# Two layers of a hybrid decoder trunk: v, gate and output projections in pairs of column groups, as 2x2 block products with seven multiplications

## The chip, the cores and the metric

The kernel runs on one core of a Trainium2 chip. The metric is the device time of one execution in microseconds. Before the change three runs gave 1668.3, 1667.81 and 1663.36 us. The names of the engines in the profile are PE (TensorE's matmuls), PEld (its weight loads), DVE (VectorE), ACT (ScalarE), POOL (GpSimd) and SP (SyncE, which here only issues DMAs).

## The reference

S = 512 tokens, width 2048, two layers, all float32. Per layer:

```
h   = rms_norm(x, pre_g)
z   = h @ w_in                       # 2048 -> 6656 = 13 groups of 512 columns
rq, rk, rv, rg (768 each), dq, dk, dv, dg (512 each), lx, lg (768 each) = split(z)
A   = retention(rope(rq), rope(rk), rv)    # 6 heads x 128, chunks of 128, then norm
B   = diff_attention(rope(dq), rope(dk), dv)   # 4 heads, causal, then norm
C   = rg_lru(causal_conv4(lx))             # 768 channels
mix = concat(A * silu(rg), B * silu(dg), C * gate(lg))
x   = x + rms_norm(mix @ w_out, post_g)    # 2048 -> 2048 = 4 groups of 512 columns
```

So there are 17 projections of 512 x 2048 by 2048 x 512 per layer, and the mixers between them.

## The kernel before, in words

Each float32 matrix is split into a high part in the float32r format and the rest (`whi`, `wlo` for weights; `hhi`, `hlo` for the normalised input; `mhi`, `mlo` for the mixers' outputs), and a product is three matmuls: high by high, high by low, low by high. K is cut into 16 tiles of 128. A weight chunk holds two of these tiles by 512 columns (a DMA of 512 KB into `raw`); `load_chunk` splits it with one ACT copy (L163) and one DVE subtraction (L164).

A `Pass` is one projection: 8 chunks by 4 PSUM banks, 192 matmuls of 128 x 512 (L208). In form A the weights are stationary and a bank holds 128 columns for all 512 tokens; in form B the activations are stationary and a bank holds 128 tokens by 512 columns. `run_pass` goes chunk by chunk over the banks and finishes the banks one after the other in the last two chunks, so that `evac` of one bank overlaps the next. `ensure` loads chunks ahead, with high priority.

The order of the passes in a layer: dv, dq, dk, three of lx and lg, three of rq and rk, three of rv and rg, dg, then four column groups of the output projection. Layer 1's dv pass begins with two of its four banks (`defer`), and the last column group is done as two halves of two banks each. Work of the mixers is written as generators in the queue `side`; `pump` takes a step of the first of them after every second chunk and bank, `drain` empties the queue ahead of the output projection (`i == 13`). SP issues in program order. For the other engines a list scheduler fixes one order per engine when the kernel is built, and each engine then takes its instructions in that order.

Names that the change touches: `evac_rvg` and `evac_dv` take v and gates from PSUM into tiles that stay in SBUF; `ret_head` is one head of retention, `ret_final` multiplies its output `ro` with the gate `rg` (L713, POOL) and transposes it; `diff_final` does that for differential attention (`dT`, L552); `lru_final` for the recurrence; `evac_y` and `finish` square, scale and add the residual, and transpose blocks of 128 tokens (`hT`) into the next layer's `hhi`, `hlo`; `start_h` and `start_norm` prepare layer 0, with `rstd` on POOL (L317).

Of the kernel before, what the change touches and what calls it, by code (L numbers as in the profile page):

```python
# [23 lines left out]
P = 128  # L24
# [12 lines left out]
NU = 77  # L37
WBUFS = 3
NWARM = 9
NPOOL = 4  # L40
LEAD, SLEAD, RLEAD = 4, 8, 6
DEFER = 3
# [3 lines left out]
C_RQ, C_RV, C_RG, C_DQ, C_DK, C_DV, C_DG, C_LX = 0, 1536, 2304, 3072, 3584, 4096, 4608, 5120  # L46
# [42 lines left out]
class Pass:  # L89
    def __init__(self, form, wsrc, kts, banks, act, evac, defer=False):  # L90
        self.form, self.wsrc, self.kts = form, wsrc, kts
        self.banks, self.act, self.evac, self.defer = banks, act, evac, defer
# [3 lines left out]
def tile_hybrid_trunk(ctx, tc, x, xt, pos, ppar, lamqk, w_in, gw, w_out, postg, cp, cm, out):  # L96
# [31 lines left out]
    xs = dp.tile([S, DM], F32, name="xs")  # L128

# [17 lines left out]
    passes = []  # L147
    chunk_list = []
    chunk_tiles = {}
# [3 lines left out]
    def load_chunk(i):  # L153
        p, c = chunk_list[i]
        raw = wp.tile([P, 2, S], F32, tag="raw", name=nm("raw"))
        hi = wp.tile([P, 2, S], F32R, tag="whi", name=nm("whi"))
        lo = wp.tile([P, 2, S], F32R, tag="wlo", name=nm("wlo"))
        src = p.wsrc[c].rearrange("p (k c) -> p k c", k=2)
        for a, b in (((0, 1), (1, 2)) if i == 0 else ((0, 2),)):
            if i == 0:  # L160
                load_xt(a)
            nc.sync.dma_start(raw[:, a:b, :], src[:, a:b, :])
            last_copy[0] = A.copy(hi[:, a:b, :], raw[:, a:b, :])  # L163
            V.tensor_tensor(lo[:, a:b, :], raw[:, a:b, :], hi[:, a:b, :], op=ALU.subtract)  # L164
        chunk_tiles[i] = (hi, lo)

    def ensure(i):
        while loaded[0] <= min(i, len(chunk_list) - 1):
            with tc.high_priority(HP):
                load_chunk(loaded[0])  # L170
            loaded[0] += 1
# [16 lines left out]
    cbase = [0]  # L188

    def run_pass(p):  # L190
        nb = len(p.banks)
        ps = {b: pb.tile([P, S], F32, tag="big", name=nm("big")) for b in p.banks}
        nch = len(p.kts) // 2
        base = cbase[0]
        cbase[0] += nch
        cnt = {b: 0 for b in p.banks}
        total = len(p.kts) * 3

        def mm(c, b):
            hi, lo = chunk_tiles[base + c]  # L200
            for kk in range(2):
                ah, al = p.act[p.kts[2 * c + kk]]
                for wt, at in ((hi, ah), (hi, al), (lo, ah)):
# [4 lines left out]
                    T.matmul(ps[b], lhsT=lhsT, rhs=rhs, start=(cnt[b] == 0), stop=(cnt[b] == total - 1))  # L208
                    cnt[b] += 1
            if cnt[b] == total:  # L210
                with tc.high_priority(HP):
                    p.evac(b, ps[b])

        order = []
        rest = 0
        if p.defer:
            order += [(c, b) for c in range(DEFER) for b in p.banks[:2]]
            order += [(c, b) for b in p.banks[2:] for c in range(DEFER)]
            rest = DEFER
        tail = nch - (2 if nb == 4 else 3)  # L220
        for c in range(rest, tail):
            order += [(c, b) for b in p.banks]
        for b in p.banks:
            order += [(c, b) for c in range(tail, nch)]
        for n, (c, b) in enumerate(order):
            ensure(base + max(c, n // nb) + 2)
# [3 lines left out]
        for c in range(nch):  # L230
            del chunk_tiles[base + c]
# [294 lines left out]
    def evac_dv(st):  # L526
        def f(tb, ps):
            t = U("dv")
            A.activation(t, ps, AF.Identity, scale=rstd[:, tb:tb + 1])
            st["dv"][tb] = t  # L530
        return f

# [12 lines left out]
    def diff_final(l, st):  # L545
# [3 lines left out]
        for h in range(DIFF_H):  # L549
# [3 lines left out]
            hi, lo = U("mhi", F32R), U("mlo", F32R)  # L553
            A.activation(hi, ps, AF.Identity, scale=subg[:, l:l + 1])
            V.scalar_tensor_tensor(lo, ps, subg[:, l:l + 1], hi, op0=ALU.mult, op1=ALU.subtract)
            st["mix"][6 + h] = (hi, lo)
# [89 lines left out]
    def lru_final(st):  # L646
        for t in range(LRU_T):
            m = st["lh"][t]
            V.tensor_tensor(m, m, st["lg"][t], op=ALU.mult)
            hi, lo = U("mhi", F32R), U("mlo", F32R)  # L650
            A.copy(hi, m)
            V.tensor_tensor(lo, m, hi, op=ALU.subtract)
            st["mix"][10 + t] = (hi, lo)
# [3 lines left out]
    def ret_head(l, st, h):  # L657
        q, k, v = st["rq"][h], st["rk"][h], st["rv"][h]
# [44 lines left out]
        del st["rq"][h], st["rk"][h], st["rv"][h]  # L703
# [6 lines left out]
    def ret_final(st, heads):  # L710
        for h in heads:
            o = st["ro"].pop(h)
            G.tensor_tensor(o, o, st["rg"][h], op=ALU.mult)  # L713
# [3 lines left out]
            hi, lo = U("mhi", F32R), U("mlo", F32R)  # L717
            A.copy(hi, ps)
            V.tensor_tensor(lo, ps, hi, op=ALU.subtract)
            st["mix"][h] = (hi, lo)  # L720
# [3 lines left out]
    def evac_rvg(st, items):  # L724
        def f(tb, ps):
            gl = [j for j, (kind, h) in enumerate(items) if kind == "g"]
            if gl:
# [322 lines left out]
```

## Time and profile before

| | |
|---|---|
| three runs | 1668.3, 1667.81, 1663.36 us (median 1667.81) |
| the profiled execution: its own time, its span | 1666.37 us, 1664.4 us |
| mean granted TensorE clock | 0.993 |
| PE, PEld busy | 1634.2 us (98%), 1349.5 us (81%) |
| DVE, ACT, POOL busy | 928.7 us (56%), 626.0 us (38%), 259.1 us (16%) |
| DMA | 177.50 MB, mean 107 GB/s |

The span is the time from the first to the last instruction. Busy times of PE come from matmuls that overlap in its pipeline, so the distance from start to start in the chain of waits prices a matmul better than the mean duration of its group. In a row of a tile's view three numbers stand for shortest, median and longest duration in ns. In a row of the stretch view each engine's busy us is followed by its number of instructions, then come the granted clock, the share of DMA engines busy and GB/s.

### The profile page before, as it was taken

To read this page: it belongs to the slowest core of one execution; us is meant where nothing else is said; L and a number is where in the kernel's file an instruction comes from. 1 tells how busy PE (TensorE), PEld (TensorE's weight loads), DVE (VectorE), ACT (ScalarE), POOL (GpSimd) and SP (SyncE) were. 2 spreads that over 40 slices of the span, in tenths; PEclk is the share of its full clock that TensorE was granted. 3 is DMA by queue.
4 is the path that set the end of the run, shared out by engine and by line. 5 is a ranking of instruction groups with operands and counts; after the bars stand their busy time and mean duration, and the time that the engine had idled before them with its cause. 6 is when DMAs were issued, how large, how long until landed. Compare 5 with 4: busy or idle time off the path is not lost. (4 is left out here: it accounts for less than half of the span.)

```text
span 1664.4 us, 19440 instructions
## 1 busy us (share of the span) xinstructions
PE 1634.2 (98%) x7541; PEld 1349.5 (81%) x7541; DVE 928.7 (56%) x1474; ACT 626.0 (38%) x966; POOL 259.1 (16%) x216
## 2 busy tenths in 40 slices
PE   9999899999999999999999998999999999999997
PEld 7788788787877888888888887888888888888886
DVE  6767765665674444322772776664677544442336
ACT  6232345457212323222662224346541222332233
POOL 0011400111261110000110131003035301100003
PEclk9999999999999999999999999999999999999999
DMA  7233222232322222344643222222323322223635
GB/s 258 79 92 101 89 64 84 89 96 76 102 76 77 76 89 83 107 146 158 222 159 100 89 89 77 76 84 83 92 86 102 101 73 77 91 96 108 196 124 199
DMA packets 54747, 177.50 MB, mean 107 GB/s; under 512 B 6656, under 2 KB 7680, under 8 KB 54656
## 3 DMA queue, kind: packets, MB, share of 16 engines
q1 hardware_dynamic: 52592, 169.94, 32.2%
q0 software_dynamic: 1920, 6.29, 1.0%
q8 instruction: 59, 0.97, 0.2%
q14 instruction: 32, 0.26, 0.1%
q10 hardware_dynamic: 144, 0.04, 0.0%
HBM read 167.86 MB, written 8.39 MB: 106 GB/s over the span
## 5 line engine op out<-in xcount | busy, mean ns | idle before, releaser
L164 DVE TENSOR_TENSOR wlo<-raw,whi 128x1024 fp32r<-128x1024 f32 (+1 forms) x289 | 370.5, 1286 | 426.7 <-ACT whi L163 412.8
L163 ACT CAST whi<-raw 128x1024 fp32r<-128x1024 f32 (+1 forms) x289 | 302.6, 1049 | 630.2 <-PE big L208 549.1
L208 PE MATMUL big<-hhi,whi 128*128 128x512 f32 x1024 | 402.9, 394 | 1.5 <-DVE lx L635 1.5
L208 PE MATMUL big<-hhi,wlo 128*128 128x512 f32 x1024 | 400.6, 391 | 1.6 <-DVE wlo L164 1.6
L208 PE MATMUL big<-hlo,whi 128*128 128x512 f32 x1024 | 400.0, 391 | 0.0
L208 PE MATMUL big<-whi,hhi 128*128 128x512 f32 x640 | 255.3, 401 | 3.7 <-ACT rv L738 2.6
L208 PE MATMUL big<-wlo,hhi 128*128 128x512 f32 x640 | 252.0, 395 | 2.7 <-DVE wlo L164 2.7
L208 PE MATMUL big<-whi,hlo 128*128 128x512 f32 x640 | 251.6, 393 | 0.0
L208 PEld LDWEIGHTS big<-hhi,wlo 128*128 128x128 f32 x1024 | 192.9, 188 | 42.5 <-DVE wlo L164 2.0
L208 PEld LDWEIGHTS big<-hhi,whi 128*128 128x128 f32 x1024 | 193.0, 188 | 41.7 <-DVE lx L635 2.0
L208 PEld LDWEIGHTS big<-hlo,whi 128*128 128x128 f32 x1024 | 193.0, 189 | 38.8
L208 PE MATMUL big<-wlo,mhi 128*128 128x512 f32 x512 | 199.5, 390 | 0.6 <-DVE wlo L164 0.6
L208 PE MATMUL big<-whi,mlo 128*128 128x512 f32 x512 | 199.8, 390 | 0.0
L208 PE MATMUL big<-whi,mhi 128*128 128x512 f32 x512 | 199.8, 390 | 0.0
L208 PEld LDWEIGHTS big<-wlo,hhi 128*128 128x128 f32 x640 | 121.5, 190 | 29.4 <-DVE wlo L164 3.1
L208 PEld LDWEIGHTS big<-whi,hhi 128*128 128x128 f32 x640 | 121.5, 190 | 28.3 <-ACT rv L738 3.0
L208 PEld LDWEIGHTS big<-whi,hlo 128*128 128x128 f32 x640 | 121.6, 190 | 24.2
L208 PEld LDWEIGHTS big<-wlo,mhi 128*128 128x128 f32 x512 | 96.1, 188 | 21.2 <-DVE wlo L164 1.5
L208 PEld LDWEIGHTS big<-whi,mlo 128*128 128x128 f32 x512 | 96.2, 188 | 19.7
L208 PEld LDWEIGHTS big<-whi,mhi 128*128 128x128 f32 x512 | 96.1, 188 | 19.6
L773 POOL TENSOR_TENSOR ry<-sy,mhalf 128x1 f32<-128x1 f32 x8 | 4.7, 585 | 406.7 <-DVE sy L771 406.7
L471 ACT ACTIVATE pr<-sc,mx 128x128 f32<-128x128 f32 (+3 forms) x64 | 33.3, 525 | 75.7 <-DVE mx L468 75.6
(212 smaller groups left out, 1530.0 us busy)
## 6 DMA issues: line engine op xcount, KB each, us to landing
raw<-in_w_in SPq DMA_DIRECT2D x207, 512.0 KB, 3.6
raw<-in_w_out SPq DMA_DIRECT2D x80, 512.0 KB, 3.5
xT<-in_xt SPq DMA_DIRECT2D x16, 256.0 KB, 6.6
xr<-in_x SPq DMA_DIRECT2D x16, 256.0 KB, 5.5
xs<-y POOLq DMA_DIRECT2D x16, 256.0 KB, 3.5
xr<-xs SPq DMA_DIRECT2D x16, 256.0 KB, 5.5
pg<-in_postg SPq DMA_DIRECT2D x8, 256.0 KB, 3.9
out<-y POOLq DMA_DIRECT2D x8, 256.0 KB, 4.5
```

Of the source, the lines that this page charges most:

```text
L163: last_copy[0] = A.copy(hi[:, a:b, :], raw[:, a:b, :])
L164: V.tensor_tensor(lo[:, a:b, :], raw[:, a:b, :], hi[:, a:b, :], op=ALU.subtract)
L208: T.matmul(ps[b], lhsT=lhsT, rhs=rhs, start=(cnt[b] == 0), stop=(cnt[b] == total - 1))
L471: A.activation(p[:, :n], sc[c][:, :n], AF.Exp, bias=mx[:, c:c + 1], scale=0.125, accum_out=sums[:, h:h + 1])
L773: G.tensor_tensor(st["ry"][tb], ms, mhalf[:, :1], op=ALU.pow)
```

## The change

Two column groups of 512 with the same activations form a `Pair`: (dv, rv heads 0 to 3), (rg heads 0 to 3, rv and rg of heads 4 and 5), and in w_out (0, 1) and (2, 3); two input and two output pairs per layer, eight in all. For a pair the product is seen as 2 x 2 blocks: the activations by halves of tokens (256) and of K (1024), the weights by halves of K and the two column groups. Seven block products are made in place of eight, in the order of `UNITS`: A11 B11, A12 B21, S1 T1, S2 T2 and S4 B22 taken by turns, S3 T3, A22 T4, each in four chunks of two K tiles. A unit is one chunk of one product for two banks of 128 tokens: 12 matmuls. S1 to S4 are sums of activation blocks, T1 to T4 sums of weight blocks.

The weight sums are made on the way in (`load_pair_unit`): the first K tile of a chunk is added on POOL (L220), the second on DVE, and then split in halves of 128 x 512. The activation sums are made by `Sums.make`: per sum and chunk two additions of 128 x 256 (four where a block is there only as high and low part) and the low part's subtraction on POOL (L364 to L367, L382), the high part on ACT (L381), and both go to DRAM (from ACT's and POOL's DMA queues, L384) and are read back by SP ahead of each unit that needs them, once in each of the two pairs that share them. For layer 1's input the first of the four sums per chunk is made on DVE. The products are combined from PSUM on DVE, with copies c1 and c5 on ACT.

Around it: all passes of the mixers are reordered (layer 0: dq, the two input pairs, dk, three of lx and lg, three of rq and rk by pairs of heads, dg, the two output pairs; layer 1 begins with the two input pairs), v and gates of the pairs go through DRAM (`vg`) and are read back per head, the next layer's input is transposed by halves of tokens (`turn`), NU falls from 77 to 75 tiles, and raw weights get 4 buffers in place of 3. `defer` and the halved last column group are gone.

The diff, cut to its core:

```diff
+A11_B11, A12_B21, S1_T1, S2_T2, S4_B22, S3_T3, A22_T4 = range(7)
+UNITS = ([(A11_B11, c) for c in range(4)] + [(A12_B21, c) for c in range(4)] + [(S1_T1, c) for c in range(4)]
+         + [(s, c) for c in range(4) for s in (S2_T2, S4_B22)]
+         + [(S3_T3, c) for c in range(4)] + [(A22_T4, c) for c in range(4)])
...
+    def load_pair_unit(p, s, c):
...
+            sums = U("sh", F32R), U("sl", F32R)
...
+                nc.sync.dma_start(sums[part].bitcast(F32), p.sums.dram[SUM_OF[s], c, part])
...
+                raw = load_raw(w2[c] if s == S1_T1 else w2[c + 4] if s == S2_T2 else w1[c + 4])
...
+                for kk in range(2):
+                    (G, V)[kk].tensor_tensor(p.x[c][kk], p.x[c][kk], raw[:, kk, :], op=ALU.add)
+            for kk in range(2):
+                split(hi[:, kk, :], lo[:, kk, :], p.x[c][kk])
...
+            raw, more = load_raw(w2[c]), load_raw(w2[c + 4])
+            for kk in range(2):
+                (G, V)[kk].tensor_tensor(raw[:, kk, :], raw[:, kk, :], more[:, kk, :], op=ALU.add)
+                split(hi[:, kk, :], lo[:, kk, :], raw[:, kk, :])
...
+    def run_pair(p, begin=()):
...
+            if s == A11_B11:
+                c1[t] = U("c1")
+                A.copy(c1[t], x)
+            elif s == A12_B21:
+                e = U("e")
+                V.tensor_tensor(e, x, c1[t], op=ALU.add)
+                o1(t, e)
...
+            elif s == S2_T2:
+                V.tensor_tensor(c1[t], x, c1[t], op=ALU.subtract)
+                V.tensor_tensor(c5[t], c5[t], c1[t], op=ALU.add)
...
+        for n, (s, c) in enumerate(UNITS):
...
+            ensure(base + n + 3)
...
+            pump(2)
...
+        def make(self, c, n, eng):
...
+            hi, lo = U("sfh", F32R), U("sfl", F32R)
+            A.copy(hi, t)
+            eng.tensor_tensor(lo, t, hi, op=ALU.subtract)
+            for part, (q, x) in enumerate(((nc.scalar, hi), (nc.gpsimd, lo))):
+                q.dma_start(self.dram[n, c, part], x.bitcast(F32))
...
+    def mixed(l, st, k, m):
...
+        if all(n in st["mf"] for n in (2 * c, 2 * c + 1, 2 * c + 8, 2 * c + 9)):
+            side.appendleft(st["sums_out"].chunk(c, G))
...
+    def start_sums():
+        for c in range(4):
...
+            st["sums_in"].make(c, 0, G)
+            yield
+        yield from st["sums_in"].rest(G)
...
-            side.append(chain(start_norm(), lead(LEAD), tables(), layer_params(0), layer_params(1), ready()))
+            side.append(chain(start_norm(), start_sums(), tables(), layer_params(0), layer_params(1), ready()))
...
-            if i == 13:
+            if i >= 11:
                 drain()
```

How this moves instructions, at three places. First POOL's order early in layer 0. Before, `rstd` is followed by small powers of the parameters (L334, L346) and the first rotary product of dq:

```order
L317 TENSOR_TENSOR rstd<-ms_429,mhalf 128x4
L334 TENSOR_TENSOR e_868<-two_865,dots_846 128x2
L346 TENSOR_TENSOR u_899<-two_865,na_895 128x6
L334 TENSOR_TENSOR e_982<-two_979,dots_962 128x2
L405 TENSOR_TENSOR qk_806<-qk_806,cos_d 128x512
```

After, behind `rstd` (row 13) come 64 rows of the 16 activation sums; here are the last five of them and the first two weight additions of the first pair (`sf` is a sum, `sfl` its low part, `wx` a weight tile, `raw` the other chunk):

```order
L367 TENSOR_TENSOR sf_834<-xT_179 128x256
L384 DMA sums_in_81<-sfl_829 128x512
L367 TENSOR_TENSOR sf_834<-xT_185 128x256
L382 TENSOR_TENSOR sfl_838<-sf_834,sfh_837 128x512
L384 DMA sums_in_81<-sfl_838 128x512
L220 TENSOR_TENSOR wx_523<-wx_523,raw_849 128x512
L220 TENSOR_TENSOR wx_539<-wx_539,raw_887 128x512
```

The first weight addition of the first pair moved behind all 16 sums of the layer's input.

Second, TensorE at the start of the output projection of layer 0. Before, the last transposes of differential attention (`dT`) stand next to the first matmuls of the first column group, and nothing of retention is left:

```order
L552 MATMUL dT_5090<-cmt,dod_1822 128x128
L552 MATMUL dT_5090<-cmt,dod_2020 128x128
L552 MATMUL dT_5090<-cmt,dod_2286 128x128
L208 MATMUL big_5110<-whi_4997,mhi_3433 128x512
L208 MATMUL big_5110<-whi_4997,mlo_3434 128x512
L208 MATMUL big_5110<-wlo_4998,mhi_3433 128x512
L208 MATMUL big_5110<-whi_4997,mhi_3456 128x512
L208 MATMUL big_5110<-whi_4997,mlo_3457 128x512
L208 MATMUL big_5110<-wlo_4998,mhi_3456 128x512
```

After, in the first output pair, between the last matmuls of its second unit, stand retention of heads 2 to 5 and the transposes `rT` of the heads before (`kv`, `ro`, `rs`, `rk` are retention's products):

```order
L345 MATMUL big_5865<-whi_5336,mlo_4863 128x512
L876 MATMUL kv_5466<-rvg_5451,kn_5464 128x128 x3
L887 MATMUL ro_5474<-rvg_5451,sT_5462 128x128 x2
L345 MATMUL big_5865<-wlo_5337,mhi_4862 128x512
L890 MATMUL ro_5474<-rst_5470,qk_4705 128x128
L887 MATMUL ro_5474<-rvg_5451,sT_5462 128x128
L890 MATMUL ro_5474<-rst_5470,qk_4705 128x128
L887 MATMUL ro_5474<-rvg_5451,sT_5462 128x128
L890 MATMUL ro_5474<-rst_5470,qk_4705 128x128
L919 MATMUL rT_5495<-cmt,ro_5135 128x128 x4
L919 MATMUL rT_5509<-cmt,ro_5236 128x128 x4
L862 MATMUL rs_5578<-qk_4995,qk_5009 128x128 x4
```

The mixers' last work moved from earlier passes into the first units of the output pair.

Third, POOL ahead of the output projection of layer 0. Before, the gate products (L713) are followed by the first power of the output norm:

```order
L713 TENSOR_TENSOR ro_4261<-ro_4261,rg_4690 128x512
L713 TENSOR_TENSOR ro_4364<-ro_4364,rg_4692 128x512
L713 TENSOR_TENSOR ro_4491<-ro_4491,rg_4694 128x512
L713 TENSOR_TENSOR ro_4572<-ro_4572,rg_4696 128x512
L773 TENSOR_TENSOR ry_6060<-sy_6058,mhalf 128x1
L800 DMA xs<-y_5318 128x512
```

After, the sums of the last chunk of mixer outputs (`mf`) and then the first weight addition of the output pair, with 66 rows from the gate powers of heads 2 and 3 (row 206) up to it:

```order
L382 TENSOR_TENSOR sfl_5820<-sf_5816,sfh_5819 128x512
L367 TENSOR_TENSOR sf_5825<-mf_5759 128x256
L384 DMA sums_out_83<-sfl_5820 128x512
L367 TENSOR_TENSOR sf_5825<-mf_5770 128x256
L382 TENSOR_TENSOR sfl_5829<-sf_5825,sfh_5828 128x512
L384 DMA sums_out_83<-sfl_5829 128x512
L220 TENSOR_TENSOR wx_5322<-wx_5322,raw_5956 128x512
L220 TENSOR_TENSOR wx_5338<-wx_5338,raw_5982 128x512
```

The weight addition moved behind the last activation sum of the operand.

More of the change, by code (lines that the diff above doesn't have):

```diff
@@ L36 @@
 EPS = 1e-6
-NU = 77
+NU = 75
 WBUFS = 3
+RBUFS = 4
 NWARM = 9
@@ L144, in tile_hybrid_trunk, with load_raw @@
     A.activation(ones, ones, AF.Identity)
-    passes = []
-    chunk_list = []
-    chunk_tiles = {}
+    units = []
+    unit_tiles = {}
     loaded = [0]
     last_copy = [None]
[L153 to L165, printed above, removed]
+    def load_raw(src):
+        raw = wp.tile([P, 2, S], F32, tag="raw", name=nm("raw"), bufs=RBUFS)
+        nc.sync.dma_start(raw, src.rearrange("p (k c) -> p k c", k=2))
+        return raw
@@ new lines, in split_tiles, with split, load_first @@
+    def split_tiles():
+        return (wp.tile([P, 2, S], F32R, tag="whi", name=nm("whi")),
+                wp.tile([P, 2, S], F32R, tag="wlo", name=nm("wlo")))
+    def split(hi, lo, raw):
+        last_copy[0] = A.copy(hi, raw)
+        V.tensor_tensor(lo, raw, hi, op=ALU.subtract)
+    def load_first(p):
+        src = p.wsrc[0].rearrange("p (k c) -> p k c", k=2)
+        raw = wp.tile([P, 2, S], F32, tag="raw", name=nm("raw"), bufs=RBUFS)
+        hi, lo = split_tiles()
+        for a in range(2):
+            load_xt(a)
+            nc.sync.dma_start(raw[:, a:a + 1, :], src[:, a:a + 1, :])
+            split(hi[:, a:a + 1, :], lo[:, a:a + 1, :], raw[:, a:a + 1, :])
+        return hi, lo
@@ L207, in mm @@
                         lhsT, rhs = at[:, b * P:(b + 1) * P], wt[:, kk, :]
-                    T.matmul(ps[b], lhsT=lhsT, rhs=rhs, start=(cnt[b] == 0), stop=(cnt[b] == total - 1))
-                    cnt[b] += 1
-            if cnt[b] == total:
+                    T.matmul(ps[b], lhsT=lhsT, rhs=rhs, start=(c == kk == n == 0), stop=(c == 7 and kk == 1 and n == 2))
+            if c == 7:
                 with tc.high_priority(HP):
                     p.evac(b, ps[b])
[L214 to L224, printed above, removed]
+        order = [(c, b) for c in range(6) for b in range(4)]
+        order += [(c, b) for b in range(4) for c in (6, 7)]
         for n, (c, b) in enumerate(order):
-            ensure(base + max(c, n // nb) + 2)
+            ensure(base + max(c, n // 4) + 2)
             mm(c, b)
@@ L234, in tile_hybrid_trunk, with halves @@
+    def halves(x):
+        return x[:, :256], x[:, 256:]
     cos_r = const.tile([P, S], F32, name="cos_r")
@@ L864, in tile_hybrid_trunk @@
[L864 to L871 removed]
+            (A_(G_LX, ev_l(st, 0)), [lambda st=st, l=l: lru_half(l, st, 0)]),
@@ L877, in tile_hybrid_trunk @@
         layer_passes.append(seq)
         for p, _ in seq:
-            passes.append(p)
-            for c in range(len(p.kts) // 2):
-                chunk_list.append((p, c))
+            for u in (UNITS if isinstance(p, Pair) else range(8)):
+                units.append((p, u))
     st = states[0]
```

403 lines of the change are left out of this document (273 added, 130 removed).

## The prediction

> **What bounds the kernel now.** I read the busy table first, then the chain of waits, then the stretch views and the groups of the engines that the change loads.
>
> ```profile
> span 1664.4 us, 19440 instructions
> PE 1634.2 (98%) x7541; PEld 1349.5 (81%) x7541; DVE 928.7 (56%) x1474; ACT 626.0 (38%) x966; POOL 259.1 (16%) x216
> 1203.45 122.41 PE big L208 x540
> 1325.85 0.89 PE rs L661 x8
> 0.00:1664.40 1664.40, 1529.79 (x6528) 0.99 0.33 107
> PE big L208 <- DVE wlo L164: 4.9, 4, 2.7
> ```
>
> The reader sees an engine that hardly waits. The second line is the whole span; the third is a piece of the chain of waits in which 540 projection matmuls follow each other, 122.41/540 = 0.2267 us from start to start (their own durations overlap, so the mean of a group is no price). The fourth prices the small 128x128 matmuls: 0.89/8 = 0.11. The fifth is the projection matmuls alone, 6528 of them: 6528 x 0.2267 = 1480 of the 1664 us. The longest kind of wait for a split weight costs 4.9 us in all. So TensorE is the bound, and a matmul taken away is worth 0.2267 us, as long as the engines that feed it stay ahead. DVE has 44% free, POOL 84%.
>
> **Removed: matmuls.** A pair of column groups took 2 x 192 matmuls and now takes 28 units of 12, that is 336. Eight pairs: 8 x 48 = 384 fewer; the order of the instructions shows 6144 instead of 6528, and all other TensorE rows as before. Gain: 384 x 0.2267 = 87.1 us. A unit is 12 x 0.2267 = 2.72, a pair 76.2. Weight loads stay under the matmuls as now.
>
> **Added: what feeds them.** The prices:
>
> ```profile
>   L164 DVE TENSOR_TENSOR wlo<-raw,whi x289: 684/1225/2321, 6.5 to 1648.9; 128x1024 fp32r<-128x1024 f32 x144, 128x512 fp32r<-128x512 f32 x1
> L439 DVE TENSOR_TENSOR qk<-big,rsb x40: 677/691/692, 92.9 to 1280.3; 128x512 f32<-128x512 f32 x40
> L400 DVE TENSOR_TENSOR rt<-qk,sin_r x24: 686/1666/1692, 424.7 to 1297.2; 64x512 f32<-64x512 f32 x24
> L401 POOL TENSOR_TENSOR qk<-qk,cos_r x24: 1288/1746/2342, 425.5 to 1300.0; 128x512 f32<-128x512 f32 x24
> L404 DVE TENSOR_TENSOR rt<-qk,sin_d x64: 678/682/690, 107.3 to 996.3; 32x512 f32<-32x512 f32 x64
> L258 DVE SCALAR_TENSOR_TENSOR ang<-turn,ang 128x512 f32<-128x512 f32 x18 | 12.4, 691 | 0.5
> L316 DVE TENSOR_SCALAR ms<-dss 128x4 f32<-128x4 f32 x8 | 1.4, 169 | 0.3
> L713 POOL TENSOR_TENSOR ro<-ro,rg x12: 1282/1291/1306, 564.7 to 1438.1; 128x512 f32<-128x512 f32 x12
> L697 POOL TENSOR_TENSOR rf<-rss,mhalf x12: 1007/1008/1019, 522.1 to 1406.3; 128x4 f32<-128x4 f32 x12
> L800 POOL DMA_DIRECT2D xs<-y x16 | 9.0, 561 | 16.9 <-DVE hlo L813 11.5 <-DVE y L797 5.4
> L584 ACT CAST xh<-xc 128x512 fp32r<-128x512 f32 x12 | 7.4, 620 | 18.9 <-DVE xc L582 18.9
> 52.46 1.03 POOL L317 TENSOR_TENSOR rstd<-ms,mhalf 128x4 f32<-128x4 f32 x1 [6.67 <-DVE ms L316]
> ```
>
> In rows with three numbers these are shortest, median and longest in ns. A 128x512 operation of DVE is 0.69, of POOL 1.29, a POOL DMA issue 0.56, an ACT copy 0.62. A 128x256 POOL addition is in no row: half of 1.29 is 0.65, the smallest POOL tensor operation that works on 4 columns is 1.01; I take 0.70, since it is nearer to half of the row of its own kind, and keep 0.65 and 1.01 as ends.
>
> One activation sum (`make`) is then two additions of 0.70, a wait for ACT's copy (0.62 and a hand-over, 0.8 together), a subtraction of 1.29, and a DMA issue of 0.56: 4.05 us on POOL; with the copy hidden behind the neighbouring sum's additions 3.25. There are 16 per operand and four operands. POOL also adds half of each weight sum, and POOL takes its instructions in the order shown: **the first weight addition of a pair stands behind all activation sums that precede it.** The splits of that unit on ACT and DVE, and so TensorE's S1 matmul, wait for it; behind SP's reads of the sums stand the weight loads of the later units. This is what decides, place by place.
>
> *(1) Layer 0, first pair.* The 16 sums can start when the pow of the last row above ends, 53.5 us. 16 x 4.05 = 65, so 118; addition, copy and subtraction (1.29 + 0.62 + 0.69) give S1 at 121.
>
> ```profile
> L208 PE MATMUL big<-hhi,wlo x1024: 387/389/628, 57.8 to 1279.2; 128*128 128x512 f32 x171
> 40.00:90.00 50.00, 48.56 (x211) 40.03 (x210) 35.88 (x55) 14.63 (x22) 4.04 (x3) 0.93 0.28 88
> 740.00:790.00 50.00, 50.00 (x222) 41.44 (x221) 15.27 (x21) 13.11 (x21) 0.00 (x0) 1.00 0.49 162
> ```
>
> The first pass ends where the second begins, at 57.8, and the eight units before S1 last 21.8: TensorE could take S1 at 79. It waits 42 (29 with 3.25 per sum: 53.5 + 52 + 2.6 = 108). From S1 on DVE has, by the order, 16 weight additions (11), 36 half splits of 0.684 (25), 14 evacuations of 0.69 (10), the angle tables (18 x 0.691, and 10 others, 20 in all), 69 small ones of 0.17 to 0.2 (13) and the rotary rows of four heads (16 x 0.682 and more, 19): 98, 102 with hand-overs, against 20 units of 2.72 = 54: 47 more. Together 89; the low end is 56 (29, and 27 if the tables move into the stall). The second row shows that this stretch had DVE at 35.88 of 50 us before; there is little cover.
>
> The L400 row gives the upper end. Alone that operation takes 686 ns, but its median is 1666, with POOL's L401 beside it (which itself goes from 1288 to 1746), while the operation fed from PSUM (L439) has 677, 691 and 692. So each meeting may cost DVE 1.666 - 0.686 = 0.98, and the order puts about 20 POOL operations into this stretch: 20 more, 109. I take none of it, since the splits' median (1225 for two halves of 684) shows no such cost, and keep 20 for the range. The Trainium skill, "SBUF — State Buffer", section "Who interferes with whom", calls it an exclusive lock: DVE's second port is POOL's only one, and one of the two holds it for a whole instruction. The L400 row agrees with that. By that rule the term would be 20 x 1.29 = 26 higher and the sum 1912.
>
> *(2) The first output pair, in both layers.* Before, the last heads' work lay between the projection matmuls of 13 earlier passes and was hidden. Now retention of heads 2 to 5, their products with the gate and the transposes of the differential heads stand in TensorE's order between the first 24 big matmuls, and POOL must do, ahead of the first weight addition: 8 rotary products and sums and 6 gate products and 12 split halves (26 x 1.29 = 33.5), 24 half-width additions (16.8), 4 pow (4.0), 12 DMA issues (6.7): 61. With the hand-overs to TensorE, ACT and DVE of twelve sums and of four heads that follow one another (12 x 0.8 and four heads' matmul, ACT, DVE, pow rounds of 5 to 6 us) S1 starts 94 after the pair does; TensorE has 21.8 of units and about 100 small matmuls x 0.11 = 11, so 33. It waits 61, of which I take 55, for what POOL can start during the pass before; ends 40 (no hand-overs) and 63. Two layers: 110 (80 to 126).
>
> *(3) Second output pair, layer 0.* In S3 and A22 DVE has 25.4 and 12.4 (evacuations, y, transposed blocks of the next layer) against 14.5 and 10.9 of TensorE: 12 (5 to 20).
>
> *(4) Layer 1's first pair.* It has no pass ahead of it any more. Its activation sums need the last token's rows; four are made on DVE, the other 12 on POOL with four half additions each: 48 x 0.70 + 12 x 1.29 + 12 x 0.56 = 56, hand-overs 10, begun 25 after the last output matmul (DVE has y and the low parts of the last two blocks of tokens first), and 2.6: S1 at 93, where TensorE, whose first 8 units need only the first half of the tokens, could take it at 26 (21.8 and the transposes). 67, of which I take 60, since the first of the twelve needs only the first of DVE's four (45 to 75). Before, the first pass of the layer begins with two banks (`defer`), and TensorE had work there in 9.65 of 10 us:
>
> ```profile
> 815.00:825.00 10.00, 9.65 (x49) 7.67 (x48) 9.13 (x18) 8.55 (x23) 2.77 (x5) 1.00 0.91 327
> ```
>
> *(5) Within the eight pairs.* S3 loads two chunks and a sum per unit, 1.57 MB in 2.72 us, 578 GB/s.
>
> ```profile
> 15.00:20.00 5.00, 5.00 (x24) 4.14 (x23) 4.73 (x7) 4.11 (x7) 0.00 (x0) 1.00 1.04 398
> ```
>
> The busiest stretch moved 398 GB/s. Four such units need 15.8 instead of 10.9 us; the lead of two to three units covers about half: 3 per pair, 24 (0 if the lead covers all, 56 if the splits too run late).
>
> *(6) The ends.* The last two blocks of tokens come only 6 matmuls apart, so DVE's and SP's rows after the last matmul grow by 4 (0 to 6). After each long wait TensorE's clock falls: the second window row above has 0.93 granted after a short idle at 49 to 54 us, 0.07 x 50 = 3.5 us; with four long waits up to 14; I take 8, since part of a slow stretch falls on matmuls that wait anyway (0 to 20).
>
> At nothing: ACT's 858 to 1225 instructions (626 to about 815 us of a longer span; the cover is its idle half); the v and gate rows through DRAM (read one head ahead); the transposes by halves of tokens, same count.
>
> Sum, against the profiled execution's own time 1666.4 (its span and 2.0; 1.4 below the median of the runs): 1666.4 - 87.1 + 89 + 110 + 12 + 60 + 24 + 4 + 8 = **1886**. Low ends: 1666.4 - 87.1 + 56 + 80 + 5 + 45 = 1765. High ends: 1666.4 - 87.1 + 109 + 126 + 20 + 75 + 56 + 6 + 20 = 1991.
>
> **Rivals.** *Throttled throughout:* DVE and POOL exclude each other in all pairs. By the order, the two have 108 us of instructions in layer 1's second output pair against 76 of TensorE, 102 against 80 in layer 0's, 82 and 79 against 76 in the second input pairs, and 20 more in (1): 32 + 22 + 6 + 3 + 20, less the 12 already counted = 71, so 1957. For it: L400's median; the page just named would make it the rule. Against it: TensorE's waits of (1) to (4) leave DVE time to catch up.
> *The waits are small:* POOL's sums fit beside the units before S1, with hand-overs hidden and half additions at 0.65. Then the low ends hold: about 1765.
> *Faster:* the sums are done in time at all four starts, since POOL would begin them as soon as their tiles are there, in the passes before; then only (5) and (6) stand: 1666.4 - 87.1 + 36 = 1615. For it: POOL is 84% idle. Against it: the order, in which the sums stand last ahead of the weight additions, and in (1) the tile that starts them ends at 53.5. It decides where the four starts cost less than 51 together.
> That matmuls are not removed is excluded by the order's count.
>
> **How the numbers follow.** Sum as worked out 0.70; throttled 0.14; small waits 0.10; faster 0.05; a balance near nothing 0.01. The range reaches from the low ends, 1765, to the throttled case and a little over, 1975; the likeliest case alone spans about 1820 to 1945. What can be told from no change is 0.3%, 5 us. Slower 0.94, same 0.01, faster 0.05.
>
> **What would show it.** 6144 big matmuls at 0.227 outside the waits; TensorE waits of 40 us and more at the first S1 of the first input pair, twice at the first output pair and once at layer 1's start, released by a split that in turn waited for POOL; POOL busy without a gap ahead of each; activation sums of about 4 us each; DVE at 90% and over in the first pair's last 20 units. Wrong I would be if TensorE reaches S1 in step with POOL, if a 128x256 POOL addition took well under 0.65, or if the weight waits sit evenly in all units.

## The result, and the profile after

The changed kernel takes 2003.61 us (median of 4 runs, 2002.0 to 2006.66) against 1665.59 us for the kernel before on the same chip: ratio 1.2032, 95% interval 1.2001 to 1.2064. Slower, as forecast, but 118 us more than the 1886 that was forecast and 29 above the range's end. (Some later comparisons have another median for the kernel before, 1663 to 1666.) The page of the changed kernel, its span, busy times and the granted clock:

```profile
span 2000.4 us, 21327 instructions
PE 1633.0 (82%) x7157; PEld 1312.9 (66%) x7157; DVE 1291.3 (65%) x1902; ACT 795.7 (40%) x1297; POOL 681.5 (34%) x636
PE   9636798999999973599752889999999999438894
PEclk9768799999999996699876899999999999768997
```

TensorE is busy 82% of a longer span, and the last two rows (busy tenths and granted clock in 40 slices of 50 us) show where it is not: slices 2 to 5, 15 to 17, 20 to 23, 35 to 36 and the last. These are layer 0's first input pair, its first output pair, the change of layers with layer 1's first input pair, layer 1's first output pair, and the end.

The place is found by TensorE's matmul starts. The time from a stage's first projection matmul to the next stage's first, less 0.2267 for each big and 0.112 for each small matmul in it, is what TensorE stopped or ran slow there (to within some 1 us):

| us lost | before | changed | forecast |
|---|---|---|---|
| layer 0, first input pair (P1) | | 103 | 92 |
| second input pairs, both | | 22 | 6 |
| first output pairs, both (O1) | | 175 | 116 |
| second output pairs, both (O2) | | 39 | 18 |
| layer 1, first input pair | | 89 | 63 |
| whole kernel, without the tail | 55 | 470 | |

(The forecast's 3 us per pair for loads is counted in each row.) Of the 415 us lost more, 384 x 0.2267 = 87 come back by the matmuls saved, and the tail after the last matmul grew by 9: 337, where the spans differ by 2000.4 - 1664.4 = 336.

The three kinds of stop are seen in the waits. TensorE in the first output pair of layer 0 (us in total, times, longest; from 724 to 834), and in layer 1's first pair (1007 to 1122):

```profile
PE rs L862 <- POOL qk L583: 23.1, 1, 23.1
PE big L345 <- ACT whi L188: 16.8, 1, 16.8
PE dT L755 <- ACT mf L757: 13.6, 1, 13.6
...
PE big L345 <- ACT whi L188: 49.6, 2, 42.6
PE rsb L552 <- DVE rb L551: 13.3, 2, 9.4
```

In layer 0's first pair POOL's order does what was forecast. From the timeline of POOL in layer 0 (start, duration, instruction, idle time before): the first and the last sums of the layer's input, and the first weight addition.

```profile
47.87 1.03 POOL L494 TENSOR_TENSOR rstd<-ms,mhalf 128x4 f32<-128x4 f32 x1 [7.94 <-DVE ms L493]
48.87 1.40 POOL L367 TENSOR_TENSOR sf<-xT,xT 128x256 f32<-128x256 f32 x2
51.00 1.28 POOL L382 TENSOR_TENSOR sfl<-sf,sfh 128x512 fp32r<-128x512 f32 x1 [0.73 <-ACT sfh L381]
...
115.55 1.26 POOL L382 TENSOR_TENSOR sfl<-sf,sfh 128x512 fp32r<-128x512 f32 x1 [0.73 <-ACT sfh L381]
117.10 0.56 POOL L384 DMA_DIRECT2D sums_in<-sfl  x1 [0.30 <-POOL sfl L382]
117.68 1.27 POOL L220 TENSOR_TENSOR wx<-wx,raw 128x512 f32<-128x512 f32 x1
```

16 sums from 48.87 to 117.66 are 4.30 each (forecast 4.05). But ACT's order holds too, which was not forecast. ACT in the first output pair, at its last sums: each cast `sfh` waits 3.31 us for POOL's additions, and the weight casts `whi`, whose data was there, follow only behind the last of them (of their four tiles two had landed by 812.8, the others by 818.1 and 822.6).

```profile
816.34 0.62 ACT L381 CAST sfh<-sf 128x512 fp32r<-128x512 f32 x1 [3.31 <-POOL sf L367]
816.99 0.33 ACTq L384 DMA_DIRECT2D sums_out<-sfh  x1
820.26 0.62 ACT L381 CAST sfh<-sf 128x512 fp32r<-128x512 f32 x1 [3.31 <-POOL sf L367]
820.91 0.33 ACTq L384 DMA_DIRECT2D sums_out<-sfh  x1
824.19 0.62 ACT L381 CAST sfh<-sf 128x512 fp32r<-128x512 f32 x1 [3.31 <-POOL sf L367]
824.84 0.33 ACTq L384 DMA_DIRECT2D sums_out<-sfh  x1
825.20 2.18 ACT L188 CAST whi<-wx 128x512 fp32r<-128x512 f32 x4 [0.40 <-ACT sfh L381]
```

SP is a third queue of this kind already here: it could load those tiles only from 806.4 to 819.6, since it waited for tiles that were still being written to DRAM as sums (first row; 755 to 825). And in this pair POOL's order is not what holds the first weight addition: POOL was done at 827 and then idle for 10.43 us, until the weights came (second row).

```profile
SPq L214 <- DMA sums_out<-sfh: 16.2, 4, 4.5
837.43 1.28 POOL L220 TENSOR_TENSOR wx<-wx,raw 128x512 f32<-128x512 f32 x1 [10.43 <-DMA raw<-in_w_out]
```

### The profile page after: what moved, and what is told of

Same layout as the page of the kernel before. It is cut to its first block, busy times and chain, and to the rows that moved or that the text cites. A ratio compares the mean times of both kernels' runs of the same rounds, so it can differ in the third digit from the quotient of the medians.

```text
span 2000.4 us, 21327 instructions
## 1 busy us (share of the span) xinstructions
PE 1633.0 (82%) x7157; PEld 1312.9 (66%) x7157; DVE 1291.3 (65%) x1902; ACT 795.7 (40%) x1297; POOL 681.5 (34%) x636
## 5 line engine op out<-in xcount | busy, mean ns | idle before, releaser
L345 PE MATMUL big<-whi,sh 128*128 128x512 f32 x512 | 212.6, 415 | 116.7 <-ACT whi L188 113.3
L189 DVE TENSOR_TENSOR wlo<-wx,whi 128x512 fp32r<-128x512 f32 x256 | 217.2, 877 | 108.8 <-ACT whi L188 105.6
L188 ACT CAST whi<-wx 128x512 fp32r<-128x512 f32 x256 | 150.1, 618 | 204.1 <-DVE wx L220 120.9
L345 PE MATMUL big<-wlo,sh 128*128 128x512 f32 x512 | 208.0, 417 | 26.7 <-DVE wlo L189 26.4
L220 POOL TENSOR_TENSOR wx<-wx,raw 128x512 f32<-128x512 f32 x96 | 144.4, 1510 | 215.6 <-DMA raw<-in_w_out 118.7
L345 PE MATMUL big<-whi,sl 128*128 128x512 f32 x512 | 208.8, 408 | 0.0
L345 PEld LDWEIGHTS big<-whi,sh 128*128 128x128 f32 x512 | 101.8, 199 | 146.2 <-ACT whi L188 123.1
L345 PEld LDWEIGHTS big<-whi,sl 128*128 128x128 f32 x512 | 102.0, 199 | 21.3
L381 ACT CAST sfh<-sf 128x512 fp32r<-128x512 f32 x64 | 39.6, 619 | 186.2 <-POOL sf L367 127.1
L345 PE MATMUL big<-whi,mhi 128*128 128x512 f32 x192 | 77.3, 403 | 33.7 <-ACT whi L188 33.7
L382 POOL TENSOR_TENSOR sfl<-sf,sfh 128x512 fp32r<-128x512 f32 x60 | 79.9, 1331 | 69.8 <-ACT sfh L381 69.7
L345 PE MATMUL big<-whi,hhi 128*128 128x512 f32 x192 | 80.6, 420 | 23.7 <-ACT whi L188 23.6
L220 DVE TENSOR_TENSOR wx<-wx,raw 128x512 f32<-128x512 f32 x96 | 84.3, 878 | 23.5 <-DMA raw<-in_w_in 23.5
```

The costliest lines, as they stand in the source:

```text
L188: last_copy[0] = A.copy(hi, raw)
L189: V.tensor_tensor(lo, raw, hi, op=ALU.subtract)
L220: (G, V)[kk].tensor_tensor(p.x[c][kk], p.x[c][kk], raw[:, kk, :], op=ALU.add)
L345: T.matmul(ps[s, t], lhsT=at, rhs=wt[:, kk, :], start=(c == kk == m == 0), stop=(c == 3 and kk == 1 and m == 2))
L381: A.copy(hi, t)
L382: eng.tensor_tensor(lo, t, hi, op=ALU.subtract)
```

## The experiments

Theory A: the activation sums, slow and serial on POOL, hold the weights through queues that take their instructions in order. Rivals: DVE and POOL lock each other and that alone makes the waits; the sums' way through DRAM or the DMA rate; the reordering of the mixers. Times of the experiments are medians of 2 runs (the last: 4), beside the kernel before on the same chip.

**Weight sums on DVE.**

```diff
-                    (G, V)[kk].tensor_tensor(p.x[c][kk], p.x[c][kk], raw[:, kk, :], op=ALU.add)
+                    (V, V)[kk].tensor_tensor(p.x[c][kk], p.x[c][kk], raw[:, kk, :], op=ALU.add)
```

> The changed kernel with all weight sums on DVE, none on POOL. Theory (the activation sums in POOL's queue hold the weight sums behind them, and ACT's copies of those sums hold the weight casts): the single waits of 23 us (layer 0) and 43 us (layer 1) at the first S1 shrink to under 10 and 25, since the additions no longer stand behind the 16 sums; the first output pairs keep their 87 us each, because there TensorE stops before S1; DVE gets 128 more operations of 0.68 = 87 us and is late more often inside the pairs. Sum 1950 to 1990. Rival (POOL and DVE lock each other, and that is what makes all waits): DVE's durations fall to their undisturbed values and the waits inside all pairs shrink, under 1930. Rival (the sums' way through DRAM is late, not the additions): the first S1 waits stay at 23 and 43, 2000 to 2060.

1966.03, in the expected range, but not in the expected way: the first S1 still waited 20.7 and 40.8 us, and the weight casts stood on ACT behind `sfh`, though their additions were done. In layer 0 (DVE's two additions, ACT's last sum, the two casts of these weights):

```profile
103.94 2.36 DVE L220 TENSOR_TENSOR wx<-wx,raw 128x512 f32<-128x512 f32 x2 [9.53 <-DMA raw<-in_w_in]
116.03 0.62 ACT L381 CAST sfh<-sf 128x512 fp32r<-128x512 f32 x1 [3.31 <-POOL sf L367]
117.10 1.14 ACT L188 CAST whi<-wx 128x512 fp32r<-128x512 f32 x2 [0.45 <-ACT sfh L381]
```

So POOL's order alone is not the holder. Nor is it the exclusion of DVE and POOL alone (that rival had under 1930). The gain of 38 is spread over all eight pairs. DVE's splits of weight sums in the changed kernel (behind the bar: busy us and mean ns):

```profile
L189 DVE TENSOR_TENSOR wlo<-wx,whi 128x512 fp32r<-128x512 f32 x256 | 217.2, 877 | 108.8 <-ACT whi L188 105.6
```

and in this run:

```profile
L189 DVE TENSOR_TENSOR wlo<-wx,whi 128x512 fp32r<-128x512 f32 x256 | 177.6, 723 | 108.4 <-ACT whi L188 105.1
```

256 x (877 - 723) = 39 us of DVE went with POOL's weight additions. The Trainium skill, "SBUF — State Buffer", section "Who interferes with whom", has a DVE instruction with two SBUF inputs and a POOL instruction that reads SBUF exclude each other. The means agree with that, though the median split of the changed kernel is 683 ns: only some operations meet. That 39 is near the gain of 38 is no proof: the additions themselves also became shorter (means of 1510 ns on POOL, 706 on DVE in this run), and the two were not separated.

**No activation sums; then no sums at all.** The arithmetic of the sums is left out, the copies, writes, reads and loads stay. The lines show the core of the edit to the activation sums:

```diff
-                    minus(t[:, cols], a21, a22)
...
-            A.copy(hi, t)
-            eng.tensor_tensor(lo, t, hi, op=ALU.subtract)
+            for kk in range(2):
+                a = f[2 * c + kk][n % 2]
+                A.copy(hi[:, kk * 256:(kk + 1) * 256], a[0] if isinstance(a, tuple) else a)
```

> Leaves out the arithmetic of the activation sums: high and low part are both a plain ACT copy of one activation block; the writes to DRAM, the reads and the weight sums stay. Theory: the waits at the start of the four pairs shrink to what DVE and the mixers' own chain need: first input pair 98 to 50, first output pairs 87 to 25 each, layer 1's first pair 89 to 35, in all 2004 - 48 - 124 - 54 = 1778 (1730 to 1840). Rival (the way through DRAM and the DMA traffic): above 1950. Rival (port lock in all pairs): the inner waits (S3, A22) shrink as well, the starts stay.

> As the one before, and the weight sums are left out too (their chunks are still loaded): seven products on unsummed blocks. Theory: what is left is 6144 matmuls, the splits, the combinations and the reordered mixers: another 50 to 70 us less, 1690 to 1730, of which 1580 would be the span without any wait that the kernel before does not have. If under 1640, the sums are all there is to pay; if it stays above 1750, the reordering of the mixers and the combinations cost by themselves.

1876.71 and 1779.80. Both above what was expected. Without activation sums P1 loses 73 and O1 123 in all; without any sums P1 50, O1 105, layer 1's first pair 31, the second input pairs 2 in all, none of it in S3. In the first of these runs S1 is held for only 8.5 and 9.6 us in the first input pairs though the way through DRAM is still there, so that way is not the holder. The sums' arithmetic costs 2003.6 - 1779.8 = 224, with all that it made wait, and about 200 remain above 1580. The inner stops of the second input pairs in S3 are the weight additions and not the loads, which were all still there. The kernel without sums in layer 1's second input pair (a stretch of 70 us; busy us of each engine, clock, DMA share, GB/s):

```profile
1020.00:1090.00 70.00, 70.00 (x310) 57.95 (x310) 45.03 (x67) 32.56 (x53) 4.32 (x8) 1.00 0.90 326
```

**The holder's queues.** The high part on POOL; then its DMA there too; then also the weight sums on DVE:

```diff
-            A.copy(hi, t)
+            eng.tensor_scalar(hi, t, 1.0, 0.0, op0=ALU.mult, op1=ALU.add)
...
-            for part, (q, x) in enumerate(((nc.scalar, hi), (nc.gpsimd, lo))):
+            for part, (q, x) in enumerate(((nc.gpsimd, hi), (nc.gpsimd, lo))):
```

> The high part of each activation sum is made on POOL (or DVE where the sum is), not on ACT; nothing else. Theory: ACT's weight casts no longer stand behind copies that wait for POOL, so in the first output pairs TensorE does its first eight units beside POOL's last sums (the waits of 13.6 and 16.9 us go), 15 less in each, while POOL needs some 0.5 us more for each of 60 sums, 8 more at each start: net 1960 to 2005. Rival (ACT's order holds nothing, only POOL's work counts): 30 us longer, 2030.

> The high part of each activation sum on POOL (as in the run before) and its DMA on POOL's queue too: ACT has nothing left to do for a sum (but the scaling of layer 0's input). The run before had shown the DMA issue on ACT's queue holding the weight casts for 12.4 us in place of the copy. Theory (two queues hold the weights, ACT's by the casts, POOL's by the additions): ACT is now free, POOL is longer by about 1 us per sum and still holds the additions, so TensorE's first eight units run beside the sums but the first S1 comes later: between 1990 and 2040. If ACT's queue were the only holder: 1920 or less.

> As the run before, and all weight sums on DVE: neither ACT's nor POOL's queue holds the weights behind the activation sums. Theory: the first S1 waits (20 to 43 us) nearly go, because its own sum was written long before; first input pair 98 to 65 (DVE's tables stay), layer 1's 85 to 50, first output pairs 85 to 65 (the mixers' own chain stays): 1860 to 1900. Rival (the sums' work as such, or their way through DRAM, sets the time): 1960 or more.

2010.94, 2018.89 and 1939.57: the first between the two expectations, the second as expected, the third not (1860 to 1900). (The lines above are the edits of the second run; the first has only the upper one, the third also the edit of the first experiment.) In the first, ACT is held by the DMA issues of the parts that POOL makes:

```profile
816.07 12.40 ACTq L384 DMA_DIRECT2D sums_out<-sfh  x4
828.51 2.18 ACT L188 CAST whi<-wx 128x512 fp32r<-128x512 f32 x4 [13.67 <-POOL sfh L381]
```

In the second, ACT is free, and in the first output pair of layer 0 the second unit loses 53 us in place of 77; TensorE then goes through its first eight units and loses 15.6 just ahead of S1. The pair as a whole gains nothing (90 in place of 88), for the sums on POOL are longer and S1 waits for them.

In the third, neither ACT nor POOL holds the weights, and in the first output pairs the 13.6 and 16.8 us stops shrink to under 5. But layer 0's first S1 waited 32.5, since a third queue holds: SP stood at its reads of the sums, whose tiles come free only as the sums go on, and the next weight load is behind them. SP's wait:

```profile
SPq L208 <- POOL sf L367: 43.5, 4, 41.7
```

and SP's rows in the timeline:

```profile
106.48 0.33 SPq L208 DMA_DIRECT2D sh<-sums_in  x1
107.16 0.33 SPq L208 DMA_DIRECT2D sl<-sums_in  x1
107.58 0.37 SPq L180 DMA_DIRECT2D raw<-in_w_in  x1
```

In layer 1 that wait was 11.7 in place of 42.6.

**The drained heads.** A step of the mixers' queue after every chunk and bank: in all plain passes; the same with the edits of the third run above; in the last four plain passes.

```diff
-            if n % 2 == 1:
-                pump()
+            pump()
```

> The changed kernel, but a step of the mixers' queue after every chunk and bank of a plain pass in place of every second, so that fewer heads are left when the queue is drained ahead of the first output pair. Theory (most of the 87 us there is the left-over retention of four heads in a row, which leaving out the sums had brought only to 53): 87 to 30 in each layer, 1880 to 1910. Rival (the 87 come from the sums of the mixers' outputs alone): above 1960.

> Both edits together: activation sums wholly on POOL, weight sums on DVE, a step of the mixers' queue after every chunk and bank. Theory: the gains add where they lie in different places: 1760 to 1810, still slower than the kernel before (DVE's tables in layer 0, the start of layer 1 and the S3 units remain).

> The changed kernel, with a step of the mixers' queue after every chunk and bank only in the last four plain passes (three of q and k, and the gate of differential attention); the earlier passes keep their pace. Theory (the left-over heads make most of the first output pairs' 87 us; the run that doubled the pace everywhere had 29 there and lost it again in layer 0's first passes and in lx): 87 to 30 in both layers and nothing lost elsewhere, 1885 to 1900. Rival (the faster pace only moves the wait into the passes before): above 1960.

1990.66, 1910.93 and 1975.21; all missed, the first and the third at their rivals' times (above 1960). O1's loss fell to 61 and 59 in all from 175 (33 in the second run), as expected. Most of it came back elsewhere: with the fast pace everywhere 58, from 7, in the first pass (while P1 fell from 103 to 67) and 87, from 26, in the passes of lx and lg; with the late one 95, from 9, in the last four passes. Moving the heads moves most of the wait; 28 us were won by the late pace.

**Cover ahead of the pair.** Two plain passes before the first input pair; then with the late pace and the weight sums on DVE.

```diff
-        if l:
-            seq[0:3] = seq[1:3] + seq[0:1]
+        seq[0:5] = [seq[0], seq[4], seq[1], seq[2], seq[3]]
...
-            side.append(chain(lead(RLEAD), layer_rstd(st)))
+            side.append(chain(layer_rstd(st), st["sums_in"].rest(G)))
```

> The changed kernel, with two plain passes (dq and the first of lx) ahead of the first input pair in both layers; in layer 1 the squares and rstd come ahead of POOL's twelve sums. Theory (the sums' 65 us of serial work need a cover of as much matmul time between the operand's last row and the first S1): the first S1 waits of 23 and 43 us and the stops before them go; layer 0's 98 to 50 (DVE's tables and rotary rows still lie there), layer 1's 89 to 30, of which the new first pass, which needs all tokens, takes some 20: 1900 to 1925. Rival (the work of three queues goes on holding the weights wherever the pair lies): above 1975.

> Both edits and all weight sums on DVE. Theory: they act in different places and add: 2004 - 115 - 95 - 35 = 1759 (1740 to 1790). It is not faster than the kernel before, because what stays (the first output pairs' last sums 2 x 30, layer 0's DVE work, y and the transposes in the second output pairs 2 x 15, the additions in S3 6 each) is still more than the 87 us of the matmuls saved.

1998.21 and 1918.67; both missed, by 73 and 129. The long first S1 waits went (the longest single stop left there is 6.4 us), but the loss spread: in layer 0 the two passes and P1 lose 114 in the first of these runs, where the same three had lost 116. In layer 1 they lose 75 in place of 95, and most of these 20 us come back in layer 0's second output pair (30 in place of 21) and in the other passes of lx and lg (25 in place of 14). A stretch of 230 us, first in the first of these runs, then in the second:

```profile
60.00:290.00 230.00, 165.34 (x554) 121.07 (x554) 151.90 (x254) 90.72 (x138) 92.89 (x92) 0.81 0.49 168
60.00:290.00 230.00, 159.61 (x556) 117.60 (x557) 151.21 (x276) 92.28 (x140) 72.77 (x78) 0.81 0.50 171
```

DVE and POOL are busy 151.9 and 92.9 us of 230 in the first. That the two together are the limit there is not shown: in the second POOL has 20 us less, and the two passes and P1 still lose 111. Why cover did not help in layer 0 stays open.

**All sums on DVE.** The activation sums as below, in both layers, and the weight sums as in the first experiment; then also the late pace.

```diff
-            st["sums_in"].make(c, 0, G)
+            st["sums_in"].make(c, 0, V)
...
-            side.appendleft(st["sums_out"].chunk(c, G))
+            side.appendleft(st["sums_out"].chunk(c, V))
```

> All activation sums and all weight sums on DVE; POOL does nothing for a pair but issue DMAs. Theory A (a sum on POOL is slow and serial: about 4.3 us each in the trace, and POOL's operations stretch DVE's: the splits fell from 877 to 723 ns when POOL lost only the weight sums): a sum on DVE takes 2 x 0.4 + 0.69 and ACT's copy, 2.3, so layer 0's first S1 comes 28 earlier, layer 1's 29, the first output pairs end 20 earlier each, and DVE's other work is no longer stretched: 1966 - 28 - 29 - 40 - 10 = 1859 (1830 to 1900). Rival B (DVE and POOL together are simply full in these places, and what POOL gives up DVE cannot take): 1960 or more.

> As the run before, and a step of the mixers' queue after every chunk and bank in the last four plain passes, which alone had brought 28 (117 in the first output pairs, given back for 89 in the passes before). Theory A: 28 to 50 below the run before, 1810 to 1835, still above the kernel before. Rival B: as the run before or slower, since the passes that take the heads now have more on DVE.

1891.56, within the expectation of theory A, though DVE has all the work now; 1859.95, 25 above the expected range but better by 32. In the first, layer 0's first S1 waits 6.2 instead of 23.1, layer 1's 18.8 instead of 42.6. Splits (704 ns) and low parts (691) are near the 684 of an undisturbed operation, and DVE's busy time grew by only 37 us, while POOL's fell by 381. A line of its page and two of its groups:

```profile
PE 1619.7 (86%) x7157; PEld 1312.1 (69%) x7157; DVE 1328.7 (70%) x2234; ACT 795.3 (42%) x1297; POOL 300.4 (16%) x304
```

```profile
L189 DVE TENSOR_TENSOR wlo<-wx,whi 128x512 fp32r<-128x512 f32 x256 | 172.7, 704 | 31.3 <-ACT whi L188 28.2
L382 DVE TENSOR_TENSOR sfl<-sf,sfh 128x512 fp32r<-128x512 f32 x64 | 44.2, 691 | 37.0 <-ACT sfh L381 35.3 <-issue 1.6
```

With the late pace this is the fastest form that was run with seven products and all their sums, and still 1.118 (1.115 to 1.121) of the kernel before.

**The angle tables.** 17 of the 18 steps of the reduction left out.

> The changed kernel without 17 of the 18 steps of the angle reduction (some 15 us of DVE work in layer 0's first pair; they are left out, so the rotary tables are not those of the reference). Theory A (in the last 20 units of the first pair DVE's rows are the bound): the S3 and A22 stops of 22 and 13 us shrink by about that, 1985 to 1992. Rival (the sums and their queues hold those units too): within 3 us of the changed kernel.

1990.27, as expected in size (13), but it came out of S1 (20 to 10) and the units of S2 and S4 (7 to 3), not of S3 and A22, which lost 24 and 13 and now lose 25 and 12. The place was wrong, so the size was in part luck: DVE's rows in P1 cost about what they last, and which unit pays depends on the order.

**The reordering alone.** Each pair as two plain passes; no sums and no combinations, all else as changed, with two exceptions: ACT copies PSUM out, and the passes that stand for an input pair take a step of the mixers' queue after every chunk and bank (64 steps for two passes, where the pair took 56).

```diff
+        seq[1:3] = [plain(W[G_DV], out_dv(st)), plain(W[G_V], out_vg(l, 0, S)), plain(W[G_G], out_vg(l, 1, 0)),
+                    plain(W[G_VG], out_vg(l, 2, 256))]
```

> The changed kernel's order and bookkeeping without the seven products: each pair is two plain passes (eight block products' worth, 6528 matmuls), with no weight sums, activation sums or combinations; v and gates still go through DRAM, layer 1 starts without the two-bank start, the mixers' queue is drained ahead of the output projection, and PSUM is copied out by ACT. It prices the reordering by itself. Theory A (the sums and their combinations are the larger part, the reordering some 100 to 130 by what stayed in the first output pairs and at layer 1's start when all sums were left out): 1770 to 1800. Rival (the reordering costs next to nothing, and what stayed without sums were the combinations): under 1700. Rival (the reordering is the larger part): above 1830.

1749.95, ratio 1.0509 (1.0490 to 1.0527): 20 below the expectation. 85 us are the order of the passes: 35 and 33 at the start of the output projection, where the left-over heads run one after another without projection matmuls beside them, 11 at the start of layer 1 without `defer`, and 7 in the tail. TensorE's waits at the output projection's start in this kernel:

```profile
PE rs L860 <- POOL qk L581: 10.3, 1, 10.3
PE big L278 <- ACT whi L186: 4.7, 1, 4.7
PE rT L917 <- POOL ro L914: 4.0, 1, 4.0
```

So the 338 us are: -87 of matmuls, +85 of order, and, as what is left, +340 of sums, combinations and their queues.

## Why the prediction was off

The sign and the four places held. The mechanism, late sums that hold the weights behind them, held in kind, but not for the queue and the unit where it bites in the output pairs. Of the signs that it named three came: sums of 4.30 us, a first S1 wait of 42.6 in layer 1, and DVE busy for 106.79 us of the 117.30 from S1 to the end of layer 0's first pair (91%). Three did not: the first S1 waited 23.1 there, not 40, in the first output pairs S1 did not wait, and POOL stood idle ahead of their weight additions.

```profile
119.70:237.00 117.30, 73.56 (x240) 53.21 (x240) 106.79 (x200) 37.64 (x60) 34.66 (x27) 0.76 0.59 201
```

By its own steps:

**Gain, 87.** 6144 matmuls, at 2.72 per unit wherever nothing waits (21.76 for the eight units of S2 and S4). Held.

**(1) 89 with 3 of (5), measured 103.** S1 was forecast for 121 and came at 119.7; a sum takes 4.30 for 4.05, a half addition 0.73 for 0.70. That S1 came so near is in part luck, for the sums began at 48.87 and not at 53.5. TensorE stopped in two places ahead of S1, not one: 8.9 already in A11, behind casts that stood behind `sfh`, and 23.1 at S1. Stops and slow matmuls cost 40 before S1 (forecast 42) and 63 from S1 on, where DVE's work was forecast to cost 47 (and loads 3). With all sums on DVE these 63 were still 59, so most of them are not POOL's. The price of a sum was nearly right; the step on the holder was not, as the runs with free queues show.

**(2) 110 with 6 of (5), measured 175: the step that failed, and half of the 118 that were missed.** It had TensorE do the first eight units beside POOL's sums and stop at S1. S1 did not wait (0.3 us lost). TensorE stopped in the second unit: 23.1 for rotary rows that stand on POOL behind four sums, 13.6 for transposes' operands and 16.8 for the next weight cast, both on ACT behind `sfh`. So 18 us of units ran after POOL's work in place of beside it. The forecast had listed POOL's queue and SP's; ACT's it had put at nothing, as an idle half. The run with ACT free shows the step by itself: there the units do run beside the sums, and the stop is at S1. Per layer the 30 us are about these: POOL was done 101 us after the pair's start, so that S1 could have come at 104 and not at 94 (10); S1 came at 119 since the units and their loads stood behind it (15); and S3 and A22 lost 8, not 3 (5).

**(3) 12, measured 39 over both layers with 6 of (5).** Layer 1's S3 loses 16 as well, and 8 of that went with the weight sums off POOL; the sum had no term for it.

**(4) 60, measured 89.** S1 came 100 after the last matmul of layer 0 (forecast 93), but TensorE stopped twice: 42.6 at S1 and 28 in its first units, of which 13.3 for the transposes of `rstd` behind DVE's rows and 7 for a cast. Without any sums these first units still lost 15. Another 10 went in S3.

**(5) 24 by the load rate, 3 per pair.** S3 lost 4 to 7 us in the second input and first output pairs, where little else comes on top, and the cause was another: with all loads and no additions S3 loses nothing in the second input pairs.

**(6) 4 for the tail, 8 for the clock.** The tail grew by 9. The clock is the second large miss. Projection matmuls that follow each other without a wait, but start 0.33 to 0.65 us apart in place of 0.2267, lose about 53 us in all, 8 before: 45 more, not 8. Of the 53, 20 are in layer 0's first pair. They lie within the places above and are counted there. The row that priced the term has no idle time from 49 to 54 us, but a short wait, 16 tiny matmuls and then slow ones; and it has one stop, while the changed kernel stops again and again. The stretch with the longest stop shows the clock at 0.69:

```profile
1007.00:1122.00 115.00, 45.45 (x181) 33.42 (x180) 51.45 (x76) 44.08 (x92) 76.34 (x93) 0.69 0.55 190
```

By its rivals: "throttled throughout" gave 1957 and is not it either. It wanted 6 and 3 us in the second input pairs, which lose 13 and 9, and 22 and 32 in the second output pairs, which lose 21 and 19. It may be partly true: with the weight sums off POOL these four pairs lose 44 in all in place of 61, but that run does not separate the exclusion from POOL's longer additions. The range ended at 1975, and the measured time lies above even the sum of the terms' high ends, 1991, since every term came out above its value. They had no single cause. Queues held by sums are in (1), (2) and (4); in (3) and (5) it is partly the weight additions, in (1) DVE's own rows, and slow matmuls after stops are in every place.

Open: how the 117 us between the order-only run less 87 (1663) and the run without any sums (1780) split among combinations, half-size splits and the reads of sums. By stage they are 36 in the first output pairs, 35 and 19 in the first input pairs and 18 in the second output pairs; by cause they were not taken apart. Nor was it tried to split the first input pair in two, with plain passes between A12 and S1.

## What to carry to other kernels

Fewer matmuls pay only if what feeds them has its own cover: here each saved matmul (0.2267 us) brought 340/384 = 0.89 us in sums, combinations and waits, on engines that share queues with the weights. When a slow producer is added, list every in-order queue that its helpers pass through (here POOL's additions, ACT's copies and DMA issues, SP's reads), and ask what stands behind them in each; freeing one shows the next. Moving work to an idle engine was no gain here, where it runs at half the speed and stretches the other: all sums on the busier DVE were 112 us faster than shared with POOL. And a stop costs more than its length: TensorE's matmuls behind the stops ran slow for another 45 us in all.

## What the runs showed of the hardware

A copy with rounding of 128x512 on POOL as a tensor-scalar operation took 0.61 us, a two-operand operation of that size 1.26 (timeline of the run with free ACT and weight sums on DVE):

```profile
98.13 0.61 POOL L381 TENSOR_SCALAR sfh<-sf 128x512 fp32r<-128x512 f32 x1
98.83 1.26 POOL L382 TENSOR_TENSOR sfl<-sf,sfh 128x512 fp32r<-128x512 f32 x1
```

With the high parts made on POOL and their DMAs issued by ACT, four issues held ACT's queue for 12.4 us, as long as POOL took to make the parts. A 128x256 addition is 0.42 on DVE (all sums on DVE) and 0.73 on POOL where nothing met it.
